# The first stage of a hybrid encoder layer in a hand-written order, with 512-column value products

## The chip, the core and the metric

The kernel runs on one core of a Trainium2 chip. A core has a matrix engine (TensorE, PE in the profile, with its weight loads as PEld), a vector engine (VectorE, DVE), a scalar engine (ScalarE, ACT), a general engine (GpSimd, POOL) and SyncE (SP), which here issues every DMA. Each engine works through its own queue of instructions in order and waits on semaphores of the others. The metric is the time of one execution on the device, in microseconds (us); of several executions, the median.

## What is computed

One layer on x of 1024 tokens by 1024, in float32: an RMSNorm, one wide projection, two attention mixers, gates, an output projection and a final norm.

```python
h = rmsnorm(x, attn_norm_g)
proj = h @ w_in
(c_q, c_kv, k_rope, z_mla, q_dil, k_dil, v_dil, z_dil,
 g_mla, g_dil) = jnp.split(proj, split_points, axis=-1)
a_out = mla_attention(c_q, c_kv, k_rope, positions, mla_q_norm_g, mla_kv_norm_g, w_uq, w_ukv)
y_mla = (a_out * jax.nn.silu(z_mla)) @ w_o_mla
d_out = dilated_mixture(q_dil, k_dil, v_dil, positions)
y_dil = (d_out * jax.nn.silu(z_dil)) @ w_o_dil
merged = gate_mla * y_mla + gate_dil * y_dil
return x + merged @ w_out
```

The change touches the first part of this: `c_q`, `c_kv`, `k_rope` (416 columns, "latents"), what `mla_attention` makes of them (`q`, `k`, `v` by `w_uq` and `w_ukv`, with a rotary part), and `v_dil` (1536 columns in three head groups of 512). The projections of `q_dil`, `k_dil` and some gates follow in a "block stage".

## The kernel before

**Products in three.** A float32 operand is held as a high part (float32r, made by a cast on ACT) and a low part (operand minus high part, on DVE or POOL); `split` (L149) makes both. `mm3` (L143) adds three matmuls: high by high, high by low, low by high (L145 to L147). Results lie in PSUM, in eight banks of 128 by 512 float32.

**The first products** (`latent_proj`, L233): x transposed is loaded in 16 tiles (two halves of 512 tokens, eight chunks `kc` of 128 rows), scaled by the norm's gain and split (`load_x`, L223); the latent weights `wl` come in eight chunks of 416 columns. For each 128 tokens, eight times three matmuls of 416 columns give latents, whose squares are summed on ACT and which DVE copies to `lat`. `tables` (L287) makes sines and cosines and stores them; `token_factors` (L269) loads x by rows, sums squares on ACT, takes a reciprocal root on DVE (`rsqrt`, L199) and spreads it as a column `rcol` and, by way of a transpose and memory, as a row `R`.

**The latents** (`latents`, L339), by half: DVE scales `lat` by the factors; TensorE transposes it; `up_weights` (L326) has split `w_uq` and `w_ukv`, through a single raw buffer, with low parts on POOL; products of 512 columns follow, each evicted by ACT (high) and DVE (low) into a staging tile `mla_st`, of which there are two, and stored. These products have two PSUM banks (`8 - NB_A`).

**The values** (`dil_v`, L423): for each of three groups `g` and two quads, 256 weight columns in two loads, split with low parts on POOL; for each of eight token tiles 24 matmuls of 256 columns into one of six banks (`NB_A`), evicted with `rcol` into `dv_st` or `dv_s` and stored.

**The block sums** (`block_sums`, L461) reload x transposed, scale it on ACT, add and subtract quarters of it on POOL, and split the four results into `s0` to `s3` (casts on ACT, low parts on DVE), in four turns `kc`. The block stage (`blocks`, L650) takes a product of 512-token halves and 512-row halves in seven half-size products instead of eight, each of 12 matmuls of 512 columns, from these sums and from differences of the weights (`block_minus`, `block_operand`, five products ahead: `LEAD`).

**What sets the order.** Up to the block stage a planner orders the instructions of each engine (`schedule_with_timeline_sim`); it lets independent work pass in front of late work, so that value products are mixed with latent products. The block stage and all later stages are inside `manual_schedule()`: there each queue has the order of the text. A tile pool with `bufs=n` hands out n buffers in turn; the next use of a buffer waits for the last one's readers.

Of the kernel before, what the change touches and what calls it, by code (L numbers as in the profile page):

```python
# [19 lines left out]
S = 1024  # L20
D = 1024
# [18 lines left out]
NB_A = 6  # L40
# [21 lines left out]
class Net:  # L62
# [170 lines left out]
    def latent_proj(self, lp, wl, xp, pj):  # L233
# [9 lines left out]
        for half in range(2):  # L243
            ps = [pj.tile([128, 512], F32, name="pj") for _ in range(4)]
            todo = []
            for kc in range(8):
                self.load_x(half, kc, xp)
                if half == 0:
                    raw = wl.tile([128, 416], F32, name="wl_raw", bufs=3)
                    self.dma(raw, a["wl"][kc])  # L250
                    self.split(raw, h[:, kc], l[:, kc], nc.gpsimd if kc % 2 else v)
                for t in range(4):
                    todo.append((kc, t))
            if half:
                todo.sort(key=lambda x: x[1])
            for kc, t in todo:
                ts = slice(512 * half + 128 * t, 512 * half + 128 * t + 128)
                self.mm3(ps[t][:, :416], self.hTh[:, kc, ts], self.hTl[:, kc, ts], h[:, kc], l[:, kc], kc == 0, kc == 7)
            for t in range(4):
                i = 4 * half + t  # L260
                junk = xp.tile([128, 256], F32, name="x_junk", bufs=2)
                nc.scalar.activation(out=junk, in_=ps[t][:, 0:256], func=AF.Square, accum_out=self.lss[:, 0, i:i + 1])
                nc.scalar.activation(out=junk[:, 0:128], in_=ps[t][:, 256:384], func=AF.Square, accum_out=self.lss[:, 1, i:i + 1])
                v.tensor_copy(self.lat[:, i, 0:400], ps[t][:, 0:400])
                v.tensor_copy(self.lat[:, i, 416:432], ps[t][:, 400:416])
            if half == 0:
                v.tensor_scalar(out=self.hb, in0=self.hb, scalar1=0.5, scalar2=None, op0=ALU.mult)

    def token_factors(self, xp, pp):  # L269

        nc, a = self.nc, self.a
        ss = xp.tile([128, 8], F32, name="x_ss", bufs=1)
        for t in range(8):
            x = xp.tile([128, D], F32, name="x_in")
            self.dma(x, a["x"][128 * t:128 * t + 128, :])
            nc.scalar.activation(out=x, in_=x, func=AF.Square, accum_out=ss[:, t:t + 1])
        y = self.rsqrt(ss, 1.0 / D, xp, 8)
        nc.vector.tensor_copy(self.rcol, y)
        pt = pp.tile([128, 512], F32, name="pj")
        nc.tensor.transpose(pt[:8, :128], y, self.ident)  # L280
        row = xp.tile([8, 128], F32, name="x_row", bufs=1)
        nc.vector.tensor_copy(row, pt[:8, :128])
        self.dma(self.rs, row)
        flat = self.rs.rearrange("a b -> (a b)")
        self.dma(self.R, flat.partition_broadcast(128))

    def tables(self, tp):  # L287
# [4 lines left out]
        self.dma(pi, a["positions"].partition_broadcast(64))  # L292
        ang = tp.tile([64, S], F32, name="ang", bufs=1)
# [21 lines left out]
    def rope(self, pa, pb, cos, sin, tp):  # L315
# [3 lines left out]
        m = [tp.tile([128, 512], F32, name=f"rope_m{i}") for i in range(4)]  # L319
# [6 lines left out]
    def up_weights(self, lp):  # L326
# [5 lines left out]
        for i in range(3):  # L332
            raw = lp.tile([128, 1024], F32, name="u_raw")
            n = 768 if i < 2 else 1024
            self.dma(raw[:, :n], a["wuq"][:, 768 * i:768 * i + 768] if i < 2 else a["wukv"])
            self.split(raw[:, :n], uh[:, i] if i < 2 else kh, ul[:, i] if i < 2 else kl, nc.gpsimd)
        return uh, ul, kh, kl

    def latents(self, up, lp, tp, pj):  # L339

        nc, a = self.nc, self.a
        v = nc.vector
        uh, ul, kh, kl = up
        for half in range(2):
            c512 = slice(half * 512, half * 512 + 512)

            r = self.rcol[:, 4 * half:4 * half + 4]
            sc = tp.tile([128, 2, 4], F32, name="lat_sc")
            for i in range(2):
                v.scalar_tensor_tensor(out=sc[:, i], in0=self.lss[:, i, 4 * half:4 * half + 4], scalar=(0.5, 1.0)[i], in1=r, op0=ALU.mult, op1=ALU.mult)  # L350
                v.tensor_tensor(out=sc[:, i], in0=sc[:, i], in1=r, op=ALU.mult)
            y = self.rsqrt(sc.rearrange("p a b -> p (a b)"), 1.0 / 128, tp, 8)
            for i in range(2):
                v.tensor_tensor(out=y[:, 4 * i:4 * i + 4], in0=y[:, 4 * i:4 * i + 4], in1=r, op=ALU.mult)
            for t in range(4):
                c = self.lat[:, 4 * half + t]
                for s, f in ((slice(0, 256), y[:, t:t + 1]), (slice(256, 384), y[:, 4 + t:5 + t]), (slice(384, 448), r[:, t:t + 1])):
                    v.tensor_scalar(out=c[:, s], in0=c[:, s], scalar1=f, scalar2=None, op0=ALU.mult)
# [11 lines left out]
            cos, sin = self.cos_m[:, c512], self.sin_m[:, c512]  # L370

            k = pt
            m = tp.tile([64, 512], F32, name="rope_m0")
            n = tp.tile([64, 512], F32, name="rope_m1")
# [5 lines left out]
            st = tp.tile([128, 2, 512], F32R, name="mla_st")  # L380
            self.split(m, st[:64, 0], st[:64, 1], v)
            self.dma(self.kp[0:16, :, c512], st[0:16])
            self.dma(self.kp[16:32, :, c512], st[32:48])
# [6 lines left out]

            def scaled(src, dst):
                st = tp.tile([128, 2, 512], F32R, name="mla_st")
# [4 lines left out]

            pa, pb = up_q(slice(512, 640)), up_q(slice(640, 768))
            o1, o2 = self.rope(pa, pb, cos, sin, tp)
            scaled(o1, self.qr[0])  # L400
            scaled(o2, self.qr[1])
            for j in range(4):
                scaled(up_q(slice(128 * j, 128 * j + 128)), self.qn[128 * j:128 * j + 128])

            for j in range(4):
# [3 lines left out]
                st = tp.tile([128, 2, 512], F32R, name="mla_st")  # L409
                self.split(ps, st[:, 0], st[:, 1], v)  # L410
                self.dma(self.kn[s, :, c512], st)

            for t in range(4):
# [3 lines left out]
                st = tp.tile([128, 2, 512], F32R, name="mla_st").rearrange("p a (h x) -> p (a h) x", x=128).rearrange("p h (a d) -> p h a d", a=2)  # L417
# [3 lines left out]
                self.dma(self.mv[r0:r0 + 128], st.rearrange("p h a d -> p (h a d)"))  # L421

    def dil_v(self, g, quad, tp, pj):  # L423

        nc, a = self.nc, self.a
        w = []
        for kk in range(2):
            raw = self.wp.tile([128, 4, 256], F32, name="w_raw")
            self.dma(raw, a["wv"][g * 2 + quad, kk])
            for k in range(0, 4, 2):  # L430
                wp = (self.wp, self.wpx)[kk]
                h = wp.tile([128, 2, 256], F32R, name="w_h", bufs=4)
                l = wp.tile([128, 2, 256], F32R, name="w_l", bufs=4)
                self.split(raw[:, k:k + 2], h, l, nc.gpsimd)
                w.append((h, l))
        for t in range(8):
            ps = pj.tile([128, 512], F32, name="pj")[:, :256]
            for kc in range(8):
                wh, wl = w[kc // 2]
                sl = slice(128 * t, 128 * t + 128)  # L440
                self.mm3(ps, self.hTh[:, kc, sl], self.hTl[:, kc, sl], wh[:, kc % 2], wl[:, kc % 2], kc == 0, kc == 7)
            pv = ps.rearrange("p (h d) -> p h d", d=64)
            f = self.rcol[:, t:t + 1]
            if g < 2:
                st = tp.tile([128, 4, 2, 64], F32R, name="dv_st")
                nc.scalar.mul(st[:, :, 0], pv, f)
                nc.vector.scalar_tensor_tensor(out=st[:, :, 1], in0=pv, scalar=f, in1=st[:, :, 0].bitcast(F32), op0=ALU.mult, op1=ALU.subtract)
                x = slice(quad * 512, quad * 512 + 512)
                if g == 0:
                    dst = self.dv[0][128 * t + 64:128 * t + 192, x]  # L450
                else:
# [1286 lines left out]
```

## Time and profile before

| | |
|---|---|
| time, median of 3 runs | 1243.35 us (1240.01 to 1243.78) |
| the profiled execution | 1242.97 us, its span 1240.9 us |
| mean granted TensorE clock | 0.997 |
| first value matmul starts | 44.5 us |
| last value matmul starts | 223.22 us |
| first matmul of the block stage (`st_a`) starts | 225.43 us |

The span runs from the first to the last instruction. An engine's busy time is the sum of its instructions; a wait is idle time in front of an instruction, with what ended it.

### The profile page before, as it was taken

What the parts mean: (1) busy time and instruction counts of PE and PEld (TensorE: products, weight loads), DVE (VectorE), ACT (ScalarE), POOL (GpSimd) and SP (SyncE); (2) the same over time, 40 slices, a digit from 0 to 9 for tenths busy, and PEclk for the clock granted to TensorE, in tenths of its full rate; (3) what the DMA queues carried; (4) which work ended last, traced back from release to release, by engine and by line L of the source; (5) the groups of instructions that cost most, each with busy time, mean ns of one, the idle gap of its engine ahead of it and who ended that gap; (6) DMA issues with size and microseconds to landing.
All of it is one profiled execution on the core that took longest, in us unless ns stands there. A gap on an engine that the chain in (4) does not pass through costs nothing.

```text
span 1240.9 us, 19482 instructions
## 1 busy us (share of the span) xinstructions
PE 1206.6 (97%) x6909; PEld 1060.0 (85%) x6909; DVE 729.7 (59%) x1304; ACT 616.0 (50%) x1292; POOL 568.8 (46%) x482
## 2 busy tenths in 40 slices
PE   8989999999999999999999999999989999999997
PEld 8988999788888888888988888877878888888886
DVE  7473524466666663246566666556657767769542
ACT  7533345444343444456565656545655656654232
POOL 1361218777777777633465533415520201168322
PEclk9999999999999999999999999999999999999999
DMA  9858579365536643297889898946543445235241
GB/s 342 222 158 303 200 289 316 102 165 158 148 115 166 183 119 127 84 265 216 246 249 268 230 269 213 283 123 162 162 124 106 111 120 140 82 109 172 85 153 51
DMA packets 126416, 221.37 MB, mean 178 GB/s; under 512 B 28072, under 2 KB 60400, under 8 KB 121392
## 3 DMA queue, kind: packets, MB, share of 16 engines
q1 hardware_dynamic: 126320, 220.14, 59.8%
q8 instruction: 54, 0.88, 0.3%
q14 instruction: 42, 0.34, 0.1%
HBM read 149.24 MB, written 70.85 MB: 177 GB/s over the span
## 4 chain that ended last, share of the span: by engine, by line
PE 71%; DMA 9%; POOL 4%; issue 2%; ACT 2%; DVE 2%; SPq 1%; ACTq 0%; POOLq 0%; DVEq 0%
PE bank L145 6%; PE bank L146 6%; PE bank L147 6%; PE bank L871 3%; PE st_a L145 2%; PE st_a L147 2%; PE st_a L146 2%; PE st_d L145 2%; PE st_c L145 2%; PE st_d L147 2%; PE st_c L147 2%; PE st_c L146 2%; PE st_d L146 2%; PE bank L896 2%; PE right L145 2%
## 5 line engine op out<-in xcount | busy, mean ns | idle before, releaser
L152 POOL TENSOR_TENSOR w_l<-w_raw,w_h 128x512 fp32r<-128x512 f32 x188 | 246.1, 1322 | 231.0 <-ACT w_h L151 180.8
L151 ACT CAST w_h<-w_raw 128x512 fp32r<-128x512 f32 x188 | 112.1, 621 | 106.5 <-POOL w_raw L496 90.7
L145 PE MATMUL bank<-at_r,w_h 128*128 128x512 f32 x344 | 141.7, 412 | 0.0
L879 DVE TENSOR_TENSOR at_r<-bank,at_r 128x512 fp32r<-128x512 f32 x128 | 88.0, 688 | 82.6 <-ACT at_r L873 82.2
L146 PE MATMUL bank<-at_r,w_h 128*128 128x512 f32 x344 | 134.9, 392 | 0.6 <-POOL at_r L152 0.6
L147 PE MATMUL bank<-at_r,w_l 128*128 128x512 f32 x344 | 135.1, 393 | 0.0
L873 ACT CAST at_r<-bank 128x512 fp32r<-128x512 f32 x128 | 74.9, 586 | 75.5 <-PE bank L871 74.8
L145 PE MATMUL pj<-w_h,at_r 128*128 128x256 f32 x384 | 109.0, 284 | 0.2 <-ACT dv_s L457 0.2
L146 PE MATMUL pj<-w_l,at_r 128*128 128x256 f32 x384 | 108.9, 284 | 0.0
L147 PE MATMUL pj<-w_h,at_r 128*128 128x256 f32 x384 | 108.9, 284 | 0.0
L496 POOL TENSOR_TENSOR w_raw<-w_raw 128x512 f32<-128x512 f32 x64 | 82.9, 1295 | 0.1
L871 PE MATMUL bank<-consts,at_f 128*128 128x128 f32 x512 | 77.4, 273 | 1.6 <-ACT at_f L863 1.1
L147 PEld LDWEIGHTS bank<-at_r,w_l 128*128 128x128 f32 x344 | 64.7, 188 | 14.6
L1143 DVE TENSOR_TENSOR at_r<-bank,at_r 128x512 fp32r<-128x512 f32 x64 | 44.0, 688 | 54.4 <-ACT at_r L1139 54.2
L145 PEld LDWEIGHTS pj<-w_h,at_r 128*128 128x128 f32 x384 | 73.4, 191 | 1.3 <-ACT dv_s L457 0.6
L147 PEld LDWEIGHTS pj<-w_h,at_r 128*128 128x128 f32 x384 | 73.4, 191 | 1.0
L146 PEld LDWEIGHTS pj<-w_l,at_r 128*128 128x128 f32 x384 | 73.4, 191 | 0.7
L895 PE MATMUL bank<-at_r,at_r 128*128 128x256 f32 x256 | 67.7, 285 | 6.4 <-DVE at_f L911 3.3
L146 PEld LDWEIGHTS bank<-at_r,w_h 128*128 128x128 f32 x344 | 65.1, 189 | 9.7 <-POOL at_r L152 1.0
L145 PEld LDWEIGHTS bank<-at_r,w_h 128*128 128x128 f32 x344 | 65.1, 189 | 8.8
L896 PE MATMUL bank<-at_r,at_r 128*128 128x256 f32 x256 | 67.5, 285 | 0.9 <-DVE at_r L879 0.9
L1124 ACT ACTIVATE at_f<-at_f,at_f 128x256 f32<-128x256 f32 x128 | 64.1, 504 | 3.0 <-DVE at_f L1117 3.0
(323 smaller groups left out, 3321.6 us busy)
## 6 DMA issues: line engine op xcount, KB each, us to landing
w_raw<-wt SPq DMA_DIRECT2D x48, 512.0 KB, 4.2
at_r<-s_dq SPq DMA_DIRECT2D x32, 512.0 KB, 8.9
s_dk<-dq_st SPq DMA_DIRECT2D x80, 128.0 KB, 2.3
s_dv<-dv_st SPq DMA_DIRECT2D x32, 256.0 KB, 3.0
s_dq<-dq_st SPq DMA_DIRECT2D x64, 128.0 KB, 2.4
zt<-s_gt SPq DMA_DIRECT2D x32, 256.0 KB, 3.1
w_raw<-wv SPq DMA_DIRECT2D x12, 512.0 KB, 6.3
at_r<-s_dk SPq DMA_DIRECT2D x8, 576.0 KB, 10.1
```

The lines of the kernel that those rows point to most:

```text
L145: mm(out, lh, rh, start=start, stop=False, skip_group_check=skip)
L146: mm(out, lh, rl, start=False, stop=False, skip_group_check=skip)
L147: return mm(out, ll, rh, start=False, stop=stop, skip_group_check=skip)
L151: self.nc.scalar.copy(out=h, in_=raw)
L152: sub.tensor_tensor(out=l, in0=raw, in1=h.bitcast(F32), op=ALU.subtract)
L496: self.nc.gpsimd.tensor_tensor(out=b[out], in0=b[x], in1=b[y], op=ALU.subtract)
L871: self.nc.tensor.transpose(pt[:, o:o + 128], self.P[k, b][:, 128 * kc:128 * kc + 128], self.ident)
L873: self.nc.scalar.copy(out=h, in_=pt)
L879: self.nc.vector.tensor_tensor(out=l, in0=pt, in1=h.bitcast(F32), op=ALU.subtract)
L895: mm(out, vv[:, kc], ph[:, x], start=kc == 0, stop=False)
L896: mm(out, vv[:, kc], pl[:, x], start=False, stop=kc == 7)
L1124: nc.scalar.activation(out=p, in_=p, func=AF.Exp, scale=-1.0, bias=nm, accum_out=den)
```

## The change

The first stage moves inside `manual_schedule()` as a whole, and its order is written out in a new function `first_stage`, as 48 value parts with other work put between them.

- A value part (`v_part`) is 12 matmuls of 512 columns, for 128 tokens: half of the eight chunks `kc`, for a whole head group. Two parts make a result. Four PSUM banks hold values, four the latents.
- The value weights of a group come in two halves `s` (`v_load`, four DMAs of 256 KB each), split with low parts on POOL, and from the second half of group 1's preparations on ("late") on DVE.
- The first products keep their order; behind them on SP come the first value weights, then x by rows, then the second half of value weights. Token squares, sines, the squares of latents and the first splits are in a fixed sequence on ACT. The token row `R` is made at part 20.
- The factors of all latents are made at once, the scaling is spread over parts 2 to 9; the up weights have three raw buffers (of the five of `mla_st`) and their low parts go to DVE, at parts 5 to 7.
- The latent products are a generator: from part 6 on, 1.75 steps of it per part. The sums are another, from part 30 on, one step per part.
- Masks, `cs_d` tables, zero stores and the loads of the first block come at parts 36 to 40, the first five operands at parts 44 to 47, with low parts on DVE. The products of sin and cos with `R` and the zero stores of `s_dq` move into the block stage; its operands alternate between two pools in fours instead of one by one.

```diff
-NB_A = 6
+LATENTS_BEGIN, LATENTS_PACE = 6, 1.75
...
+        for kc in range(8):
+            self.load_x(0, kc, xp)
+            raw = wl.tile([128, 416], F32, name="wl_raw", bufs=3)
+            self.dma(raw, a["wl"][kc])
+            self.split(raw, h[:, kc], l[:, kc], nc.gpsimd if kc % 2 else v)
+            for t in range(4):
+                product(t, kc)
+            if kc == 5:
+                next(tables)
+        for kc in range(8):
+            self.load_x(1, kc, xp)
+        for t in range(4, 8):
             for kc in range(8):
...
+                product(t, kc)
...
+        self.v_load(0, 0)
+        for t in range(3):
+            load(t)
+        next(tables)
+        for t in range(4):
+            squared(t)
+            taken(t)
+        for i in range(4):
+            self.v_split(0, i, nc.gpsimd)
+        for t in range(3):
+            squares(t)
+            if t < 2:
+                load(t + 3)
+        next(tables)
+        squared(4)
+        taken(4)
+        self.v_load(0, 1)
+        for t in range(5, 8):
+            squares(t - 2)
+            load(t)
+            if t == 5:
+                next(tables)
+            if t == 6:
+                for i in range(4):
+                    self.v_split(1, i, nc.gpsimd)
+            squared(t)
+            taken(t)
+        for t in range(6, 8):
+            squares(t)
+        run_all(tables)
         y = self.rsqrt(ss, 1.0 / D, xp, 8)
...
+        raw = [tp.tile([128, 1024], F32, name="mla_st", bufs=5) for _ in range(3)]
+        size = 768, 768, 1024
+        for i, n in enumerate(size):
+            self.dma(raw[i][:, :n], a["wuq"][:, 768 * i:768 * i + 768] if i < 2 else a["wukv"])
+        yield uh, ul, kh, kl
+        for i, n in enumerate(size):
+            self.split(raw[i][:, :n], uh[:, i] if i < 2 else kh, ul[:, i] if i < 2 else kl, nc.vector)
+            yield
...
+    def v_load(self, g, s):
...
+        raws = self.v_raw[s] = [self.wp.tile([128, 2, 2, 256], F32, name="w_raw") for _ in range(2)]
+        for i in range(2):
+            for quad in range(2):
+                self.dma(raws[i][:, :, quad], self.a["wv"][2 * g + quad, s][:, 2 * i:2 * i + 2])
...
+    def v_part(self, c, pool, tp):
+
+        g, r = divmod(c, 16)
+        part, t = divmod(r, 4)
+        t += 4 * (part // 2)
+        s = (0, 1, 1, 0)[part] ^ (g & 1)
+        begin = part % 2 == 0
+        if begin:
+            self.v_ps[t] = pool.tile([128, 512], F32, name="pj")
+        ps = self.v_ps[t]
+        sl = slice(128 * t, 128 * t + 128)
+        for i in range(4):
+            kc = 4 * s + i
+            self.mm3(ps, self.hTh[:, kc, sl], self.hTl[:, kc, sl], *self.v_w[s, i], begin and i == 0, not begin and i == 3)
+        if begin:
+            return
...
+        loads(0)
+        loads(1)
+        yield
+        yield
+        scaled(0)
+        yield
+        for kc in range(4):
+            added(kc)
+            if kc:
+                parts(kc - 1)
+                if kc < 3:
+                    loads(kc + 1)
+                    yield
+            yield
+            if kc < 3:
+                scaled(kc + 1)
+                yield
+        yield
+        parts(3)
...
+            latents = self.latents(next(weights), up, tp, pl)
+            self.latent_factors(tp)
...
+            for c in range(48):
+                self.v_part(c, pj, vp)
+                g, r = divmod(c, 16)
+                if 2 <= c < 10:
+                    self.latent_scaled(c - 2)
+                if 5 <= c < 8:
+                    next(weights)
+                if c == 20:
+                    self.token_row(vp, pl)
+                first, second = (0, 1) if g & 1 else (1, 0)
+                if r == 6:
+                    self.v_load(g + 1, first)
+                if r == 14:
+                    self.v_load(g + 1, second)
+                if g < 2 and 12 <= r < 15:
+                    for i in ((0, 1), (2,), (3,))[r - 12]:
+                        self.v_split(first, i, nc.gpsimd if g == 0 else nc.vector)
+                if g and r < 3:
+                    for i in ((0, 1), (2,), (3,))[r]:
+                        self.v_split(1 - (g & 1), i, nc.gpsimd if g == 1 else nc.vector)
+                if c >= LATENTS_BEGIN and latents:
+                    steps += LATENTS_PACE
+                    while steps >= 1 and latents:
+                        steps -= 1
...
+                elif later and c >= 30:
+                    next(later, None)
+                if c == 36:
+                    self.cos_d, self.sin_d = self.table(dpool, "cs_d", 0)
...
+                if c == 40:
+                    self.block_loads(0, self.block_items[0], (self.wp, None))
+                if c >= 44:
+                    for j in ((0, 1), (2,), (3,), (4,))[c - 44]:
+                        self.block_minus(j, self.block_items)
+                        self.block_operand(j, self.block_items, nc.vector)
...
-            wp = (self.wp, self.wpx)[j % 2]
+            wp = (self.wpx, self.wp)[j // 4 % 2]
...
+            if x in (2, 3, 4, 5):
+                y, c = (self.cos_d, self.sin_d)[x // 2 - 1], slice(512 * (x % 2), 512 * (x % 2) + 512)
+                self.nc.gpsimd.tensor_tensor(out=y[:, c], in0=y[:, c], in1=self.R[:, c], op=ALU.mult)
...
+            if x in (4, 8, 12, 16):
+                i = x // 4 - 1
+                self.dma(self.dq[2][i].rearrange("e c r h (a b) f m -> (e c r) (h a) (b f m)", a=2), self.zero.unsqueeze(1).to_broadcast([128, 4, 512]))
```

More of the change, by code (lines that the diff above doesn't have):

```diff
@@ L269, in token_factors, with product @@
-    def token_factors(self, xp, pp):
-        nc, a = self.nc, self.a
-        ss = xp.tile([128, 8], F32, name="x_ss", bufs=1)
[L273 to L276, printed above, removed]
+        ps = {}
+        def product(t, kc):
+            ts = slice(128 * t, 128 * t + 128)
+            self.mm3(ps[t][:, :416], self.hTh[:, kc, ts], self.hTl[:, kc, ts], h[:, kc], l[:, kc], kc == 0, kc == 7)
@@ new lines, in first_products, with load, squares @@
+        ss = xp.tile([128, 8], F32, name="x_ss", bufs=1)
+        xs = {}
+        def load(t):
+            xs[t] = xp.tile([128, D], F32, name="x_in")
+            self.dma(xs[t], a["x"][128 * t:128 * t + 128, :])
+        def squares(t):
+            nc.scalar.activation(out=xs[t], in_=xs[t], func=AF.Square, accum_out=ss[:, t:t + 1])
+        self.v_load(0, 0)
[5 more added lines that the diff above has]
+            taken(t)
@@ L318, in rope @@
         v = nc.vector
-        m = [tp.tile([128, 512], F32, name=f"rope_m{i}") for i in range(4)]
+        m = [tp.tile([128, 512], F32, name=f"rope_m{i}", bufs=1) for i in range(4)]
         for mi, (p, tab) in zip(m, ((pa, cos), (pb, sin), (pb, cos), (pa, sin))):
@@ L345, in latents @@
             c512 = slice(half * 512, half * 512 + 512)
[L347 to L358, printed above, removed]
+            cos, sin = self.cos_m[:, c512], self.sin_m[:, c512]
             nh = lp.tile([128, 3, 512], F32R, name="lat_h", bufs=1)
@@ L389, in up_q, with stage @@
                 return ps
+            def stage():
+                return tp.tile([128, 2, 512], F32R, name="mla_st", bufs=5)
             def scaled(src, dst):
-                st = tp.tile([128, 2, 512], F32R, name="mla_st")
+                st = stage()
                 nc.scalar.mul(st[:, 0], src, QK_SCALE)
@@ L395, in scaled @@
                 self.dma(dst[:, :, c512], st)
[L398 to L401, printed above, removed]
+            pa = up_q(slice(512, 640))
+            st = stage()
+            self.split(m, st[:64, 0], st[:64, 1], v)
+            self.dma(self.kp[0:16, :, c512], st[0:16])
+            self.dma(self.kp[16:32, :, c512], st[32:48])
+            yield
+            o = self.rope(pa, up_q(slice(640, 768)), cos, sin, tp)
+            yield
             for j in range(4):
                 scaled(up_q(slice(128 * j, 128 * j + 128)), self.qn[128 * j:128 * j + 128])
+                if j > 1:
+                    scaled(o[j - 2], self.qr[j - 2])
+                yield
             for j in range(4):
@@ L486, in block_loads @@
+    def block_loads(self, n, item, pools):
+        raw = [pools[n % 2].tile([128, 8, 128], F32, name="w_raw", bufs=2) for _ in range(2)]
         for i in range(2):
@@ L650, in blocks @@
     def blocks(self, items, tp, pp):
[L652 to L654 removed]
+        pools = self.wp, tp
         places = 7 * len(items)
         steps, ps = {}, {}
[L657 to L660 removed]
@@ new lines, in run @@
+            with tc.manual_schedule(), tc.tile_pool(name="wpx", reuse_waits="tile", bufs=2, side="right") as self.wpx, tc.tile_pool(name="cosd", reuse_waits="tile", bufs=1, side="right") as dpool, ExitStack() as sums:
+                self.block_items = [(T_QK + (g * 2 + quad) * 4 + which * 2, g, quad, which) for quad in range(2) for g in range(3) for which in range(2)] + [(T_ZM + i,) for i in BLOCK_GATES]
+                cp.tile([128, 896], F32, name="masks")
+                self.masks = self.hand(2048, 896)
+                self.first_stage(cp, dpool, sums)
```

330 lines of the change are left out of this document (156 added, 174 removed).

## The prediction

> **What bounds the kernel now.** I read the page first. One core ran 1240.9 us from first to last instruction; the execution took 1242.97 us, 2.07 us outside the span; the median of the three runs is 1243.35 us, 0.38 above it.
>
> ```profile
> span 1240.9 us, 19482 instructions
> PE 1206.6 (97%) x6909; PEld 1060.0 (85%) x6909; DVE 729.7 (59%) x1304; ACT 616.0 (50%) x1292; POOL 568.8 (46%) x482
> ```
>
> TensorE is the bound, but 97% hides pipelining: a matmul's bar lasts longer than the distance to the next, so short gaps vanish. I therefore went to busy times by stretch, then to TensorE's waits up to 240 us, then to single matmuls.
>
> ```profile
> 60.00:90.00 30.00, 25.87 (x191) 24.12 (x190) 21.55 (x58) 9.93 (x18) 17.74 (x12) 1.00 0.56 174
> 180.00:210.00 30.00, 30.00 (x252) 30.00 (x252) 11.25 (x8) 16.77 (x31) 21.57 (x17) 1.00 1.00 336
> 210.00:240.00 30.00, 27.87 (x164) 24.64 (x164) 11.09 (x10) 15.24 (x29) 22.41 (x17) 0.94 0.46 154
> 240.00:270.00 30.00, 30.00 (x135) 24.82 (x134) 19.91 (x32) 11.25 (x21) 22.87 (x18) 1.00 0.44 111
> ```
>
> The columns are PE, PEld, DVE, ACT, POOL, granted clock, DMA share, GB/s. From 240 us on, in the block stage, TensorE has no gap: about 135 matmuls per 30 us. Whatever moves the start of that stage moves the end of the kernel, as long as its feeders keep up. So the change, which rewrites all that lies before, is priced by one question: when does the block stage start, and at full clock?
>
> ```profile
> PE pj L145 <- ACT wl_h L151: 5.7, 1, 5.7
> PE pj L365 <- DVE lat_l L369: 2.3, 1, 2.3
> PE st_a L145 <- ACT dv_s L457: 1.9, 1, 1.9
> PE pj L365 <- DVE lat L358: 1.5, 1, 1.5
> PE pj L145 <- DVE mla_st L394: 1.5, 1, 1.5
> PE pj L365 <- DVE mla_st L152: 0.9, 1, 0.9
> PE pj L280 <- DVE rs_y L210: 0.5, 1, 0.5
> PE pj L145 <- DVE lat_l L369: 0.3, 1, 0.3
> PE pj L145 <- ACT dv_s L457: 0.2, 1, 0.2
> ```
>
> After the first wait, for the first weights, TensorE waits 9.1 us in eight places: five around the latent work, the token row's transpose, the hand-over of a bank, the start of the block stage. The last one is in the timeline:
>
> ```profile
> 222.86 0.28 PE L147 MATMUL pj<-w_h,at_r 128*128 128x256 f32 x1
> 223.22 0.28 PE L147 MATMUL pj<-w_h,at_r 128*128 128x256 f32 x1
> 225.43 0.50 PE L145 MATMUL st_a<-at_r,w_h 128*128 128x512 f32 x1 [1.93 <-ACT dv_s L457]
> 229.88 0.39 PE L145 MATMUL st_b<-at_r,w_h 128*128 128x512 f32 x1
> 231.92 0.39 PE L145 MATMUL st_b<-at_r,w_h 128*128 128x512 f32 x1
> ```
>
> Three 256-column matmuls start in 0.36 us, **0.120 us each**. Nine of 512 columns (229.88 to 231.92) start in 2.04 us, **0.2267 us each**. The block stage begins at 225.43, and its first twelve matmuls take 4.45 us instead of 2.72: after the wait the granted clock is down (0.94 in that stretch). 1.73 us go there, so the block stage stands as if begun undisturbed at 225.43 + 1.73 = **227.2 us**.
>
> **The change, part by part.** I add up TensorE's work in the new order, with distances from start to start, and ask at each join whether an operand is late.
>
> ```profile
> L145 PE MATMUL pj<-w_h,at_r x384: 276/283/386, 44.5 to 223.0; 128*128 128x256 f32 x192
> L147 PE MATMUL pj<-wl_h,at_r x64: 346/353/548, 7.6 to 44.3; 128*128 128x416 f32 x64
> L365 PE MATMUL pj<-consts,lat x32: 270/272/328, 65.1 to 132.8; 128*128 128x128 f32 x24, 128*64 128x128 f32 x8
> 97.42 0.39 PE L146 MATMUL pj<-lat_l,uq_h 128*128 128x512 f32 x1
> 98.34 0.39 PE L147 MATMUL pj<-lat_h,uq_l 128*128 128x512 f32 x1
> 73.23 0.65 PE L365 MATMUL pj<-consts,lat 128*128 128x128 f32 x4 [2.29 <-DVE lat_l L369]
> 73.64 0.36 PE L147 MATMUL pj<-w_h,at_r 128*128 128x256 f32 x1
> ```
>
> *First products* (192 of 416 columns) end at 44.5 us now, gapless after the start. Their order stays; only the first chunk is strict now (high by high, then the two low ones, tile by tile), which makes TensorE wait once for the first low part: I add 0.3 us. 44.8.
>
> *Values*: three lines of 384 (L145, L146, L147), 1152 matmuls of 256 columns, become 576 of 512. 1152 x 0.120 = 138.2; 576 x 0.2267 = 130.6: **7.7 us less**. In the latent work, though, four 512-column matmuls start in 0.92 us (97.42 to 98.34), 0.230 each. At that pace values take 132.5. I take 0.2267, since values move weights of the same shape as the block stage, and keep 2 us for the range. The Trainium skill (TensorE: Matmul & The Clock Gate, section "Wait — 56ns, not 53.3ns?") gives N/2.4 GHz plus about 2.5 ns per warm matmul, which speaks against the wide form: by it the saving is an estimated 1.4 us instead of 7.7. Here the distances exceed N/2.4 by 13.3 ns at both widths, so the measurement decides.
>
> *Latents*: 120 matmuls x 0.230 = 27.6, and 32 transposes at 0.41/4 = 0.10, 3.3; the transpose for the token row 0.1. Unchanged: 31.0.
>
> Sum without a wait: 44.8 + 130.6 + 31.0 = **206.4**. Now the waits.
>
> *Tokens in front, late factors.* TensorE's first value parts need no token factor; the first eviction does, after part 5. 44.8 + 5 x 2.72 = 58.4. ACT's queue by then holds eight token squares (L276 below), those of the first products, two sines and eight casts of value weights; I estimate that some 8 us of it lie behind the last first product. DVE's reciprocal root is 12 operations at the 0.165 of L210. Factors near 55, latent factors (18 such operations) near 59. Token row and R move to part 20; their store and reload sit in SP's queue in front of some stores, which rings of 3 and 5 buffers cover. Scaling the latents (0.347 and 0.696 us for the two large of three operations per tile by L358's rows) is spread over parts 2 to 9, up weights (three buffers, so three loads without a turn between) over 5 to 7, low parts on DVE. Both finish just ahead of the first transposes and `up_q`; here 0 to 4 us can be lost, since DVE holds evictions, scaling, weights and low parts in a single queue. I take 1.
>
> ```profile
> L210 DVE SCALAR_TENSOR_TENSOR rs_y<-rs_u,rs_y 128x8 f32<-128x8 f32 x9 | 1.2, 165 | 0.1
> L358 DVE TENSOR_SCALAR lat<-lat,rs_y 128x256 f32<-128x256 f32 x8 | 2.8, 347 | 0.0
> L276 ACT ACTIVATE x_in<-x_in 128x1024 f32<-128x1024 f32 x8 | 8.5, 1063 | 3.2 <-DMA x_in<-x 3.2
> L358 DVE TENSOR_SCALAR lat<-lat,rs_y 128x128 f32<-128x128 f32 x8 | 5.6, 696 | 0.0
> L369 DVE SCALAR_TENSOR_TENSOR lat_l<-pj,consts,lat_h 128x512 fp32r<-128x512 f32 x6 | 4.4, 744 | 5.0 <-ACT lat_h L368 5.0
> L474 ACT ACTIVATE y<-y,consts 128x512 f32<-128x512 f32 x16 | 10.9, 718 | 2.7 <-DMA y<-xt 2.7
> L151 ACT CAST s_h<-y 128x512 fp32r<-128x512 f32 x16 | 9.8, 616 | 8.9 <-POOL y L476 2.7 <-POOL y L478 2.6 <-POOL y L479 2.2
> L152 DVE TENSOR_TENSOR s_l<-y,s_h 128x512 fp32r<-128x512 f32 x16 | 20.9, 1338 | 28.3 <-ACT s_h L151 27.9
> L479 POOL TENSOR_TENSOR y<-y,y 128x512 f32<-128x512 f32 x4 | 6.3, 1564 | 1.6 <-ACT y L474 1.4
> y<-xt SPq DMA_DIRECT2D x16, 256.0 KB, 6.5
> 221.22 0.69 DVE L152 TENSOR_TENSOR s_l<-y,s_h 128x512 fp32r<-128x512 f32 x1 [1.09 <-ACT s_h L151]
> ```
>
> *Latents woven in* (1.75 steps per part, from part 6 to 27; four banks where there were two). A step's high and low part cost ACT about 0.6 us (as for `s_h`) and DVE 0.744 (L369), and its bank is asked for again four steps, some 9 us, later. The waits on `lat_l` and `mla_st` (2.3, 1.5, 0.9, 0.3 us) have cover now. At parts 14 and 30 SP's load of value weights waits for the split that frees its buffer, and behind it queue the stores of that part and the first loads of the sums; the weights are asked for six parts later, at least 16 us. Residual 0.5.
>
> *Block sums* run in parts 30 to 43, operands of the first block in 44 to 47. One turn: loads 6.5, four scalings 2.9, four POOL adds at most 6.3 (4 x 1.564, the slowest of their lines), four casts 2.5 with DVE behind at 1.34. POOL is needed 25 us of the 49 us between part 30 and the block stage; two turns overlap (two buffers), and I get the last sums about 42 us after part 32, the block stage asking 43.5 after it. Cover of some 2 us for ACT, which has these casts ahead of the operands. I take 0.5, with 0 to 5 for the range.
>
> *Late low parts on DVE*: eight for values, five for operands. A DVE low part takes 0.69 us alone (221.22) and 1.338 on average beside POOL's adds. 13 x 1.338 = 17.4 us, beside TensorE's 54 us in parts 28 to 47; with the 16 of the sums, 39 of 54. It fits. The Trainium skill (GPSIMD Engine Reference, section "8. Key points") says that the two engines share SBUF interfaces when DVE reads two SBUF inputs, which speaks against the move; 1.338 against 0.69 agrees, and at the doubled price it still fits.
>
> *Start of the block stage*: first banks were latent banks, idle since part 27. The wait of 1.93 us and the slow clock (1.73) go. What leaves the front of the stage (four POOL products of sin and cos, four zero stores) reappears inside it: four POOL instructions like L479's, 6 us, with five operands of lead, 13.6 us. Hidden; without that cover up to 6.
>
> Sum: 206.4 + 1 + 0.5 + 0.5 = **208.4**; against 227.2 that is **18.8 us less**. I round to 18: 1242.97 - 18 = 1225.0, and by the median **1225.3 us**.
>
> **The rivals.**
> *A. The latent waits return.* In a fixed order an engine cannot pass over a late instruction; the planner's order could. Then only the wide matmuls (7.7) and the join (1.93 + 1.73) are gained: 11.4, **1232 us**. For it: DVE's queue in parts 4 to 9 is nearly full. Against: four banks instead of two.
>
> *B. DMA fills up.* Steps 9 to 18 of a half store twelve tiles of 512 KB within some 21 us, with four value stores of 512 KB and 1 MB of weights: 9 MB, 430 GB/s. The fullest stretch above moves 336 at a share of 1.00. 9 MB at 336 is 27 us: 6 us late per half, 12 in all if no ring absorbs it: 18 - 12 = 6 gained, **1237 us**. Against it: a backlog of that size fits in five staging buffers and four banks.
>
> *C. The sums end last: slower.* If the four turns follow one another with no overlap (loads wait for low parts, low parts for adds), a turn is 6.5 + 2.9 + 6.3 + 5.4 (4 x 1.338) = 21 us, four are 84, against 49 available. The block stage starts 35 us late: 18 - 35 = 17 us slower, **1260 us**. It decides from 67 us on (16.8 per turn). For it: fixed order puts evictions, sums and operands in one ACT queue, and DVE's low parts double beside POOL. Against: two buffers per tile, loads for two turns issued at once.
>
> *D. The gain is there but is eaten* by small waits of each kind: **within 3.7 us** of before.
>
> **How the numbers follow.** Forecast 0.73 (own range 1221 to 1230), A 0.12, B 0.06, C 0.05, D 0.04. A measurement tells about 0.3%, 3.7 us, from no change. Faster by more: 0.89, counting nearly all of A and B; within: 0.05; slower: 0.06. Lower end: 20.8 us less without any wait (227.2 - 206.4), and 1 us of scatter: 1221. Upper end: 2 for 0.230 and the unknown 4 and 5 are unlikely all at once; with A inside, 1234.
>
> **What would show it.** The first `st_a` matmul at 207 to 211 us with 0.2267 to the next at once and no wait on a value eviction; value matmuls 0.227 apart, 576 of them; no TensorE wait over 1 us between 45 and 205. Wrong: TensorE waiting on `lat`, `lat_l` or weights around 60 to 80 (A), ACT waiting for `mla_st` stores with TensorE behind it (B), `st_a` or `st_c` waiting on operands or sums (C), gaps inside the block stage from POOL.

## The result and the profile after

Six executions of the changed kernel have a median of **1235.51 us** (1230.85 to 1237.92), six of the kernel before 1243.57 (1240.01 to 1248.18): a ratio of 0.9926 [0.9902, 0.995], 8.1 us less where 18 were forecast, and above the 1234 at which the forecast range ended. Times of the changed kernel follow the granted clock of the execution: 1230.85 and 1232.25 at a mean of 0.997 and 0.996, 1237.92 and 1237.89 at 0.990 and 0.989. The profiled execution is the slowest of the six: 1237.92 us, its span 1236.1, its clock 0.990, against 1242.97, 1240.9 and 0.997 before.

First the page's head of the changed kernel: busy time and instructions of each engine.

```profile
span 1236.1 us, 18196 instructions
PE 1203.1 (97%) x6333; PEld 1032.8 (84%) x6333; DVE 738.0 (60%) x1286; ACT 612.1 (50%) x1268; POOL 547.2 (44%) x466
```

576 matmuls fewer (6909 to 6333), as the wider values must have it. Next TensorE's waits from 0 to 260 us: engine, what waited, for whom; total us, times, longest.

```profile
PE pj L145 <- ACT wl_h L151: 5.6, 1, 5.6
PE st_a L145 <- ACT w_h L151: 3.5, 1, 3.5
PE pj L146 <- DVE w_l L152: 0.7, 1, 0.7
PE st_a L147 <- DVE w_l L152: 0.5, 1, 0.5
PE pj L421 <- DVE lat L405: 0.4, 1, 0.4
PE pj L146 <- DVE wl_l L152: 0.2, 1, 0.2
```

Behind the first weights, eight waits of 9.1 us have become five of 5.3. The latent work waits 0.4 us where it waited 6.5. But the largest is new and stands at the join with the block stage, on an operand's cast. TensorE's timeline there (start, duration, instruction, idle time before it and its releaser):

```profile
207.45 0.39 PE L147 MATMUL pj<-w_h,at_r 128*128 128x512 f32 x1
211.34 0.79 PE L145 MATMUL st_a<-at_r,w_h 128*128 128x512 f32 x1 [3.50 <-ACT w_h L151]
...
213.05 0.79 PE L147 MATMUL st_a<-at_r,w_l 128*128 128x512 f32 x1 [0.49 <-DVE w_l L152]
213.64 0.63 PE L145 MATMUL st_a<-at_r,w_h 128*128 128x512 f32 x1
214.07 0.63 PE L146 MATMUL st_a<-at_r,w_h 128*128 128x512 f32 x1
...
218.22 0.40 PE L147 MATMUL st_b<-at_r,w_l 128*128 128x512 f32 x1
```

The last value matmul starts at 207.45, so the block stage could have begun at 207.45 + 0.23 = **207.7** (forecast: 208.4). Its fifteenth matmul would then stand at 207.7 + 14 x 0.2267 = 210.9; it stands at 218.22. **7.4 us** are lost: 4.0 in the two waits, 3.4 to the slow clock (0.43 us from 213.64 to 214.07, not 0.23): from 211.24 to 218.07 the granted clock is 0.50, and half of these 6.83 us is lost. Against before, the block stage runs 227.2 - (207.7 + 7.4) = 12.1 us ahead, not 18.8.

Who is late is read from ACT's timeline, where the casts of the operands lie behind those of the sums:

```profile
183.13 0.72 ACT L552 ACTIVATE y<-y,consts 128x512 f32<-128x512 f32 x1 [1.47 <-DMA y<-xt]
...
198.97 0.72 ACT L552 ACTIVATE y<-y,consts 128x512 f32<-128x512 f32 x1 [5.14 <-DMA y<-xt]
...
207.79 1.14 ACT L151 CAST s_h<-y 128x512 fp32r<-128x512 f32 x2 [2.22 <-POOL y L558]
209.47 0.62 ACT L151 CAST s_h<-y 128x512 fp32r<-128x512 f32 x1 [0.54 <-POOL y L559]
...
210.67 1.14 ACT L151 CAST w_h<-w_raw 128x512 fp32r<-128x512 f32 x2
```

The scaling of turns three (183.13) and four (198.97) waits for loads of `y`. SP's timeline says when these go out; the line behind it, of SP's waits from 160 to 200 us, says for whom they wait, and DVE's timeline when that work is done:

```profile
165.05 4.54 SPq L141 DMA_DIRECT2D y<-xt  x8
...
180.47 4.64 SPq L141 DMA_DIRECT2D y<-xt  x4
...
194.29 4.65 SPq L141 DMA_DIRECT2D y<-xt  x4
```

```profile
SPq L141 <- DVE s_l L152: 17.4, 4, 9.3
```

```profile
177.43 6.38 DVE L152 TENSOR_TENSOR s_l<-y,s_h 128x512 fp32r<-128x512 f32 x4 [0.42 <-ACT s_h L151]
191.72 5.91 DVE L152 TENSOR_TENSOR s_l<-y,s_h 128x512 fp32r<-128x512 f32 x4 [7.91 <-ACT s_h L151]
```

Each tile `y` has two buffers. A third turn can load only once DVE has read the first turn's tiles: low parts from 177.43, loads from 180.47; low parts from 191.72, loads from 194.29. That is the chain of rival C, at 194.29 - 180.47 = 13.8 us a turn.

The second loss is 320 us later, where attention begins. Aligned instruction by instruction, the lead of 12.1 us is kept to the end of the block stage, then falls to 7.9 (the same matmul at 546.0 before and 538.1 after), to 3.9 by 842, and is 4.8 at the end of the span. POOL's timelines at the hand-over, first of the kernel before, then of the changed one (`area` is one-element memsets that open memory for attention):

```profile
522.36 2.54 POOL L152 TENSOR_TENSOR w_l<-w_raw,w_h 128x512 fp32r<-128x512 f32 x2 [3.11 <-ACT w_h L151]
524.83 0.09 POOL L1269 MEMSET area<- 1x1 f32 x1
526.58 0.09 POOL L1269 MEMSET area<- 1x1 f32 x1 [1.66 <-PE st_a L147]
...
542.91 0.09 POOL L1269 MEMSET area<- 1x1 f32 x1 [10.01 <-DMA s_gt<-dq_st]
```

```profile
514.98 1.29 POOL L152 TENSOR_TENSOR w_l<-w_raw,w_h 128x512 fp32r<-128x512 f32 x1 [1.44 <-ACT w_h L151]
516.21 0.26 POOL L1441 MEMSET area<- 1x1 f32 x6
...
534.15 0.09 POOL L1441 MEMSET area<- 1x1 f32 x1 [13.35 <-DMA s_gt<-dq_st]
```

With a lead of 12.1 the first memset belongs at 524.83 - 12.1 = 512.7. It starts at 516.21, 3.5 us late, behind low parts whose casts on ACT come late; ACT's and TensorE's timelines of the changed kernel:

```profile
511.56 0.62 ACT L151 CAST w_h<-w_raw 128x512 fp32r<-128x512 f32 x1 [1.90 <-PE st_d L146]
514.29 0.62 ACT L151 CAST w_h<-w_raw 128x512 fp32r<-128x512 f32 x1 [2.11 <-PE st_a L146]
...
534.27 0.58 ACT L1311 CAST at_r<-bank 128x512 fp32r<-128x512 f32 x1 [6.10 <-POOL area L1441]
```

```profile
535.41 1.18 PE L1303 MATMUL bank<-consts,at_f 128*128 128x128 f32 x4 [2.72 <-ACT at_f L1296]
```

The casts wait for products of the block stage. By the code that is a wait for buffers: operands now alternate between the two pools in fours, the last four (108 to 111) all lie in the pool from which the first gate weights take theirs, and a buffer comes free only with each product. The last memset waits for a store, 13.35 us instead of 10.01. How the late low part comes to delay that store is in the chain of work that ended last, of the changed kernel from 500 to 545 us:

```profile
516.88 7.31 DMA at_r<-s_dq
524.25 9.59 DMA s_gt<-dq_st
```

The first loads of the attention go out behind the late memsets. SP waits 1.5 us for one of them to land before it sends the last store, at 524.25; in the kernel before that store went out at 534.82, so with a lead of 12.1 it belongs at 522.7. From there to the memset it takes 9.9 us instead of 8.1; why it takes longer isn't shown. ACT waits for that memset, TensorE for ACT, and the granted clock is 0.50 from 535.51 to 538.92.

### The profile page after: what moved, and what is told of

It reads as the page before. It is cut to its first block, busy times and chain, and to the rows that moved or that the text cites. A ratio compares the mean times of both kernels' runs of the same rounds, so it can differ in the third digit from the quotient of the medians.

```text
span 1236.1 us, 18196 instructions
## 1 busy us (share of the span) xinstructions
PE 1203.1 (97%) x6333; PEld 1032.8 (84%) x6333; DVE 738.0 (60%) x1286; ACT 612.1 (50%) x1268; POOL 547.2 (44%) x466
## 4 chain that ended last, share of the span: by engine, by line
PE 70%; DMA 11%; DVE 6%; issue 6%; ACT 3%; POOL 2%; SPq 1%; POOLq 0%; ACTq 0%; DVEq 0%
PE bank L145 5%; PE bank L146 5%; PE bank L147 5%; PE bank L1043 4%; PE st_a L147 2%; PE st_a L146 2%; PE st_a L145 2%; PE st_d L147 2%; PE st_c L147 2%; PE st_d L146 2%; PE st_c L146 2%; PE st_c L145 2%; PE st_d L145 2%; PE bank L1068 2%; PE bank L1067 2%
## 5 line engine op out<-in xcount | busy, mean ns | idle before, releaser
L152 POOL TENSOR_TENSOR w_l<-w_raw,w_h 128x512 fp32r<-128x512 f32 x175 | 230.7, 1330 | 215.4 <-ACT w_h L151 168.2
L145 PE MATMUL bank<-at_r,w_h 128*128 128x512 f32 x344 | 143.6, 417 | 0.0
L146 PE MATMUL bank<-at_r,w_h 128*128 128x512 f32 x344 | 136.4, 396 | 0.6 <-POOL at_r L152 0.6
L1045 ACT CAST at_r<-bank 128x512 fp32r<-128x512 f32 x128 | 74.8, 585 | 76.1 <-PE bank L1043 75.1
L146 PE MATMUL pj<-w_l,at_r 128*128 128x512 f32 x192 | 75.0, 391 | 0.7 <-DVE w_l L152 0.7
L145 PE MATMUL pj<-w_h,at_r 128*128 128x512 f32 x192 | 75.2, 392 | 0.0
L147 PE MATMUL pj<-w_h,at_r 128*128 128x512 f32 x192 | 74.8, 390 | 0.0
L1311 ACT CAST at_r<-bank 128x512 fp32r<-128x512 f32 x64 | 37.5, 586 | 58.7 <-PE bank L1303 51.7
L1043 PEld LDWEIGHTS bank<-consts,at_f 128*128 128x128 f32 x512 | 59.8, 141 | 2.7 <-ACT at_f L1035 1.5
L1067 PEld LDWEIGHTS bank<-at_r,at_r 128*128 128x128 f32 x256 | 48.4, 189 | 12.8 <-DVE at_f L1083 3.9
## 6 DMA issues: line engine op xcount, KB each, us to landing
at_r<-s_dk SPq DMA_DIRECT2D x8, 576.0 KB, 12.4
```

Source lines behind the costliest of these rows:

```text
L145: mm(out, lh, rh, start=start, stop=False, skip_group_check=skip)
L146: mm(out, lh, rl, start=False, stop=False, skip_group_check=skip)
L147: return mm(out, ll, rh, start=False, stop=stop, skip_group_check=skip)
L152: sub.tensor_tensor(out=l, in0=raw, in1=h.bitcast(F32), op=ALU.subtract)
L1043: self.nc.tensor.transpose(pt[:, o:o + 128], self.P[k, b][:, 128 * kc:128 * kc + 128], self.ident)
L1045: self.nc.scalar.copy(out=h, in_=pt)
```

## The experiments

Two causes were put against each other and against chance: the sums' loads (two buffers) at the join, and the alternation in fours at the hand-over. The first four kernels ran on one chip with the kernel before (median 1242.45 there).

**The changed kernel again**, for the comparison on this chip.

> The changed kernel itself, as the yardstick of this set. Both theories: about 8 us below the kernel before (1235 to 1236 us); TensorE waits some 3.5 us for the first operand of the block stage, and some 2.7 us for the first attention exponentials.

1234.42 us (12 executions), 0.9945 [0.9927, 0.9964]. The waits at the join are 2.1 and 1.1 us here; the last memset again waits 13.24 us.

**Alternation one by one** from operand 8 on:

```diff
-            wp = (self.wpx, self.wp)[j // 4 % 2]
+            wp = (self.wpx, self.wp)[j // 4 % 2 if j < 8 else j % 2]
```

> From the ninth operand on, operands alternate between the two pools one by one instead of in fours. Theory (the last four operands of the block stage fill the pool from which the first gate weights need two buffers, so their cast waits for a product, POOL opens the attention areas about 3.5 us late and the attention starts with a wait and a slow clock): about 4 us less than the changed kernel, the wait for the first exponentials below 0.5 us, the first block product as late as before. Rival (the loss behind the block stage is scatter of clock and DMA): no difference beyond 1.5 us, and the cast still waits.

1229.97 us, 0.9902 [0.988, 0.9925], 4.5 us below the changed kernel. The waits at the join stay (2.5 and 1.1), those at the hand-over are gone: from 500 to 560 us TensorE waits for nothing. POOL's memsets have the pattern of before again:

```profile
511.48 0.09 POOL L1441 MEMSET area<- 1x1 f32 x1
513.23 0.22 POOL L1441 MEMSET area<- 1x1 f32 x5 [1.66 <-PE st_a L147]
...
529.81 0.09 POOL L1441 MEMSET area<- 1x1 f32 x1 [10.26 <-DMA s_gt<-dq_st]
```

So the order of the operands' buffers made that loss. Aligned as above, this kernel's lead over the kernel before is 13.4 us at 500 us and 13.2 at 600; the changed kernel's beside it falls from 14.1 to 9.7.

**A third buffer for three of the four `y` tiles:**

```diff
-                    x = y[kc, i, k] = tp.tile([128, 512], F32, name=f"y{i}{k}", bufs=2)
+                    x = y[kc, i, k] = tp.tile([128, 512], F32, name=f"y{i}{k}", bufs=2 if i and k else 3)
```

> Three buffers instead of two for three of the four tiles of the block sums. Theory (loads of turn three wait for low parts of turn one on DVE, doubled beside POOL, so the sums end some 5 us late and hold ACT's queue in front of the first operands): sums end about 5 us sooner, the wait for the first operand falls from 3.5 to under 1 us, the slow clock after it goes, in all 5 to 7 us less than the changed kernel up to the block stage. Rival (POOL's adds or the loads' DMA time are the bound, not the buffer): sums end within 1.5 us of the changed kernel.

1231.41 us, 0.9915 [0.9889, 0.9941], 3.0 below the changed kernel; the two intervals overlap, so these times alone wouldn't show a gain. At the join TensorE's timeline has no wait and no slow clock:

```profile
206.95 0.39 PE L147 MATMUL pj<-w_h,at_r 128*128 128x512 f32 x1
207.18 0.39 PE L145 MATMUL st_a<-at_r,w_h 128*128 128x512 f32 x1
```

In this stage the cause is settled: the fifteenth matmul of the block stage stands at 210.35, the changed kernel's beside it at 216.22, 5.9 us later. The whole gained less than the stage. The hand-over doesn't explain that: here a memset waits 13.59 us and TensorE 3.0 on `at_f`, but the changed kernel loses about as much there. What differs in the two traces is the clock: behind 500 us this execution has five stretches of 3.41 us at half the clock, the changed kernel's two (last section).

**Both edits together.**

> Both edits. Theory: the two add, 9 to 11 us less than the changed kernel, about 1225 us, 18 us below the kernel before. Rival (one bottleneck behind both, or scatter): no better than the better of the two.

1223.42 us, 0.9845 [0.9823, 0.9868]: 11.0 below the changed kernel and 19.0 below before, more than 4.5 + 3.0. It was repeated on another chip, to see how far executions of one kernel lie apart.

> The kernel of e3_both once more, beside the repeated token experiment. 17 to 20 us below the kernel before, the first block product near 207 us.

1228.84 us in four executions (1222.95 to 1230.09), 0.9885 [0.9855, 0.9915]: 13.4 below the kernel before on that chip (1242.28), less than the 17 to 20 expected. Over both chips, the six executions at a clock of 0.996 to 0.997 took 1221.86 to 1224.19, the four at 0.992 to 0.994 took 1228.64 to 1230.33; the median of the ten is 1224.1. So the two edits together are worth some 6 to 11 us, and a split of them to the microsecond isn't to be had from times. In the trace of the repetition the last memset waits 10.20 us for the store, and the block stage begins at 207.25:

```profile
207.25 0.39 PE L145 MATMUL st_a<-at_r,w_h 128*128 128x512 f32 x1
```

The loads of its third turn go out at 171.05 instead of 180.47, and its last cast of a sum starts at 201.86 instead of 209.47.

With both losses out of the way, single parts of the change were taken back, each against this kernel; the start of the block stage is the better measure, since what comes after can't blur it. In the three traces with a third buffer it lies between 207.08 and 207.25. The first four of these kernels ran on a third chip (kernel before: 1243.52 there), so their times stand beside those of the kernel with both edits from two other chips.

**Late low parts on POOL again:**

```diff
-                        self.v_split(first, i, nc.gpsimd if g == 0 else nc.vector)
+                        self.v_split(first, i, nc.gpsimd)
...
-                        self.v_split(1 - (g & 1), i, nc.gpsimd if g == 1 else nc.vector)
+                        self.v_split(1 - (g & 1), i, nc.gpsimd)
...
-                        self.block_operand(j, self.block_items, nc.vector)
+                        self.block_operand(j, self.block_items)
```

> e3_both with the late low parts (eight of values, five of operands) on POOL again. Theory (POOL's adds of the sums are the chain that ends closest to the block stage; 13 low parts of 1.3 us are 17 us more on POOL in parts 28 to 47): the sums end later, the block stage waits, 2 to 6 us slower than e3_both. Rival (DVE is what is doubled by the sharing, POOL has room): within 1.5 us of e3_both.

1234.66 us, 0.9936 [0.9908, 0.9964]; the block stage begins at 214.64, 7.4 later, more than the 2 to 6 expected and not by the expected way. The wait isn't at the block stage: it is in the values, where a low part of the last weights lies behind the first turn's additions in POOL's queue (POOL's timeline, then TensorE's):

```profile
179.69 1.26 POOL L559 TENSOR_TENSOR y<-y,y 128x512 f32<-128x512 f32 x1
180.92 1.71 POOL L152 TENSOR_TENSOR w_l<-w_raw,w_h 128x512 fp32r<-128x512 f32 x1
```

```profile
182.68 0.79 PE L146 MATMUL pj<-w_l,at_r 128*128 128x512 f32 x1 [6.26 <-POOL w_l L152]
```

**Each value matmul as two of 256 columns:**

```diff
-            self.mm3(ps, self.hTh[:, kc, sl], self.hTl[:, kc, sl], *self.v_w[s, i], begin and i == 0, not begin and i == 3)
+            for q in (slice(0, 256), slice(256, 512)):
+                self.mm3(ps[:, q], self.hTh[:, kc, sl], self.hTl[:, kc, sl], *(x[:, q] for x in self.v_w[s, i]), begin and i == 0, not begin and i == 3, skip=True)
```

> e3_both with each 512-column value matmul as two of 256 columns, all else in place. Theory (0.120 us from start to start at 256 columns, 0.2267 at 512, TensorE without gaps): 7.7 us slower than e3_both, starts 0.120 apart. Rival (only a few ns per matmul are saved by width, or other waits hide it): under 2 us slower.

This kernel doesn't compute the layer's values any more; it is for timing alone. 1231.24 us, 0.9907 [0.9876, 0.9938]; the block stage begins at 215.18, 7.9 later than at 207.25, where 7.7 was the forecast's value of the wide form. The narrow matmuls again start 0.12 us apart, with no wait of more than 0.7 us. By the 2.5 ns per warm matmul of the Trainium skill (TensorE: Matmul & The Clock Gate, section "Wait — 56ns, not 53.3ns?") this would have been an estimated 1.4 us; the trace doesn't agree, and bears the measured distances out.

**One raw buffer for the up weights** in place of three:

```diff
-        raw = [tp.tile([128, 1024], F32, name="mla_st", bufs=5) for _ in range(3)]
...
-        for i, n in enumerate(size):
-            self.dma(raw[i][:, :n], a["wuq"][:, 768 * i:768 * i + 768] if i < 2 else a["wukv"])
+
+        def load(i):
+            raw = tp.tile([128, 1024], F32, name="u_raw", bufs=1)
+            self.dma(raw[:, :size[i]], a["wuq"][:, 768 * i:768 * i + 768] if i < 2 else a["wukv"])
+            return raw
+        raw = {0: load(0)}
...
+            if i:
+                raw[i] = load(i)
```

> e3_both with one raw buffer for the three up weights, each load behind the split of the one before. Theory (each load takes 4 to 5 us behind a split, ACT and DVE stand in order behind it, and low parts of the latents come late for the first up product): a TensorE wait around the first up products of 4 to 9 us, 4 to 9 us slower than e3_both. Rival (the fixed order has cover for it): within 1.5 us.

1237.73 us, 0.9957 [0.9931, 0.9983]; the block stage begins at 219.16, 11.9 later, more than the 4 to 9 expected: TensorE's waits come to 8.5 us, and the granted clock is 0.50 from 75.53 to 85.77. TensorE's waits from 10 to 240 us:

```profile
PE pj L145 <- ACT lat_h L429: 5.9, 1, 5.9
PE pj L145 <- DVE lat_l L430: 2.1, 1, 2.1
...
```

Here rival A is seen at work: ACT's casts of weights wait 6.09 and 5.70 us for their loads and start at 70.68 and 78.38; in the fixed order the casts of the latents stand right behind them, at 71.42 and 79.33, and TensorE waits for these.

**Tokens behind the value weights:** the first loads and squares of token rows go behind the second half of the first value weights.

```diff
-        for t in range(3):
-            load(t)
...
-        for t in range(3):
-            squares(t)
-            if t < 2:
-                load(t + 3)
...
         self.v_load(0, 1)
+        for t in range(3):
+            load(t)
+        for t in range(3):
+            squares(t)
+            if t < 2:
+                load(t + 3)
```

> e3_both with the first token loads and their squares behind the second half of the first value weights. Theory (token factors come some 8 us later, the scaling of the latents with them, and the first transposes wait): a TensorE wait on lat of 4 to 8 us near 63 us, 4 to 8 us slower than e3_both. Rival (value parts need no factor until their eviction, so it is hidden): within 1.5 us.

1235.15 us, 0.9918 [0.9892, 0.9944]. The trace of that run shows an execution of another kind (told of at the end), so the kernel was run again:

> The kernel of e7_tokens_late once more, for a trace in the usual state. Theory (late token factors delay the scaling and the first transposes): a TensorE wait on lat of 4 to 8 us near 63 us and the first block product 4 to 10 us later than in e3_again. Rival (hidden, as values need no factor before their eviction): within 1.5 us.

1233.46 us, 0.9927 [0.9906, 0.9947], 4.6 above the kernel with both edits on the same chip; the block stage begins at 213.8, 6.6 later. The factors are late, the scaled latents after them, and TensorE's transposes wait, with the slow clock behind. On `lat` they wait 2.2 us in three places, not the 4 to 8 expected; 1.32 us more in front of the first has no recorded cause:

```profile
65.86 0.30 PE L421 MATMUL pj<-consts,lat 128*128 128x128 f32 x1 [1.32 <-issue]
...
67.71 0.33 PE L421 MATMUL pj<-consts,lat 128*128 128x128 f32 x1 [0.95 <-DVE lat L405]
68.99 0.48 PE L421 MATMUL pj<-consts,lat 128*128 128x128 f32 x1 [0.95 <-DVE lat L405]
69.12 0.78 PE L145 MATMUL pj<-w_h,at_r 128*128 128x512 f32 x1
```

## Why the prediction was wrong

In the profiled executions the forecast's 18.8 us became 4.8: 18.8 + 0.7 (first stage) - 7.4 (join) - 4.2 (hand-over) - 3.1 (later). By the medians 8.1 are left, since the profiled execution of the changed kernel is its slowest.

**Right: TensorE's work in the first stage.** 208.4 was forecast for its end, 207.7 measured. The wide values were priced at 7.7 and cost 7.9 to take back. "Latents woven in" and "Tokens in front" were given 1.5 us of waits together; TensorE waits 0.4 for latents and 0.7 for a low part. Rivals A and B did not come: no latent wait over 0.4 us, no wait of TensorE for a bank. The runs with one raw buffer and with late tokens show that three buffers and early tokens keep A away (11.9 and 6.6 us).

**Right: the second step of the join.** The four POOL products moved into the block stage are hidden, as forecast; from 240 to 270 us TensorE has no gap:

```profile
240.00:270.00 30.00, 30.00 (x134) 24.85 (x133) 20.15 (x33) 13.57 (x25) 24.48 (x20) 1.00 0.83 264
```

**Wrong: "Block sums", the term of 0.5 us.** The step read "two turns overlap (two buffers), and I get the last sums about 42 us after part 32, the block stage asking 43.5 after it". Part 32 starts 16 parts of 2.72 us ahead of 207.7, at 164.2; the last sum's cast ends at 210.1, 46 us after it, and an eviction (0.68) and the operand's own cast (0.62) follow in the same queue. The step summed up what each engine is busy for and left the buffers' cycle out: two turns overlap, but the third can't load until DVE, at 1.6 us a low part, has read the first (SP waits 17.4 us for these low parts). That is rival C's mechanism for two turns of four, at 13.8 us a turn; C was set aside because it had been priced as all or nothing, with a point of decision at 16.8. Its price here isn't 35 us but 4.0, and 3.4 more because the wait brings the slow clock. The stated range of 0 to 5 held the wait and not the clock, although the prediction takes 1.93 and 1.73 for just such a pair in the kernel before.

**Wrong by omission: the end of the block stage.** "Whatever moves the start of that stage moves the end of the kernel, as long as its feeders keep up" was applied without asking whether the change touches the feeders at the far end. It does: "operands alternate between two pools in fours" is in the diff and has no term. It took 4.2 us of the lead in the profiled execution, and one by one alone gave 4.5 us back.

**The remaining 3.1 us** lie in attention. TensorE waits 2.0 us for a load of keys (`s_dk`) instead of 0.8, and two stretches at half the clock that the kernel before doesn't have, from 781.27 and from 839.29, take 1.7 us each; some 1.5 us come back behind them. Where these stretches fall differs between executions of one kernel (last section). Why the load of keys is late wasn't taken apart by a run and stays open: with both edits that wait is 3.1 and 3.2 us, and of a lead of 19.8 us behind the hand-over 14.1 and 12.4 are left at the end of the two traces.

The forecast time of 1225.3 is about reached once both losses are mended (1223.42 on one chip, 1228.84 on another), so most of the expected gain was there; two orders of buffers, at the two ends of the block stage, took it.

## What to carry to other kernels

When work is put into a fixed order, don't only add up what each engine has to do in a stretch: follow each ring of buffers once around (load, use, last reader, next load) and set the length of a turn against the time available; here 13.8 us a turn made the stage late though no engine was full. A change to the order in which buffers are handed out has its price at the last use, where another stage takes over the pool, so price both ends. And price a wait of TensorE of 2 us and more with its slow clock: here 4.0 us of waits took 7.4. How much slow clock a wait brings differs from one execution to the next, so a difference of a few us between two kernels is better read where the stage begins or ends than in the whole time.

## What the runs showed of the hardware

**The slow clock comes in stretches of 3.41 us, and a wait's length alone doesn't decide on it.** The same wait, on `at_f` in the attention, has 1.97 us in the kernel before (up to 844.33) and 1.96 in the changed one (up to 839.12). Windows of 3.41 us around it, of the kernel before and of the changed one (columns as in the prediction, the granted clock third from the right):

```profile
840.30:843.71 3.41, 2.06 (x12) 1.45 (x11) 1.84 (x3) 1.69 (x3) 3.41 (x6) 1.00 0.03 7
843.71:847.13 3.42, 2.80 (x18) 2.54 (x19) 1.99 (x3) 2.66 (x5) 2.00 (x2) 1.00 0.41 108
```

```profile
835.88:839.29 3.41, 1.45 (x7) 0.89 (x6) 2.41 (x3) 1.39 (x4) 3.31 (x5) 1.00 0.03 7
839.29:842.70 3.41, 3.41 (x13) 3.02 (x14) 2.21 (x3) 3.08 (x6) 1.27 (x1) 0.50 0.66 175
```

In the changed kernel all of the wait lies in one window (3.41 - 1.45 = 1.96 idle), and the next has half the clock, which costs 1.7 us. In the kernel before an edge cuts it into 1.35 and 0.62, and the clock stays full. These windows aren't chosen freely: in each of the eleven traces that record the clock it is 1.00 or 0.50 and changes only on a grid of 3.41 us. In the changed kernel slow stretches begin at 211.24 (two in a row), 535.51, 781.27, 839.29 and 904.15, all whole multiples of 3.413 apart. Between 12 and 1220 us of these traces, all 38 windows at full clock with 1.93 us or more of idle time on TensorE are followed by a slow one; of the others at full clock, with 1.54 us or less, only three are, behind 1.0 to 1.2 us. What makes those three differ isn't shown. The wait on `at_f` lies in one window in six traces, all slow behind it, and is cut in five, none slow.

The grid lies differently under each execution, so one kernel's executions differ: up to 1220 us the profiled execution of the changed kernel has six slow stretches, the one in the experiments three, and 3 x 1.7 = 5.1 us is what their spans are apart (1236.1 and 1231.0).

The Trainium skill (TensorE: Matmul & The Clock Gate, section "What's actually happening") has TensorE at 1.2 GHz after an idle window of about 3.4 us, counted by a free-running window. The traces agree on the free-running window and on the slow rate: 512 columns at 1.2 GHz are 0.427 us, and 213.64 to 214.07 is 0.43. That a whole window must be idle they don't bear out: 1.93 us of it sufficed in front of the block stage before.

**DVE beside POOL.** A low part on DVE takes 0.69 us alone (in the prediction's rows) and 6.38 / 4 = 1.60 beside POOL's additions (177.43), more than the average of 1.338 that the forecast used. That slowness is in the cycle that held the loads.

**One execution of another kind.** The profiled execution of the first run with late tokens took 3104.08 us. Its trace holds no record of the clock (1.00 is printed in its place); its 512-column matmuls in the block stage start some 0.6 us apart throughout. The nine other executions there took 1231.96 to 1237.91, the eight of its repetition 1229.65 to 1238.88. It is left out, and nothing here explains it.
